# Gate and u projections of a two-layer encoder in pairs, by one level of Strassen

## The chip, the cores and the metric

The kernel runs on one core of a Trainium2 chip. The core has a matrix engine (TensorE, PE in the rows), a vector engine (VectorE, DVE), a scalar engine (ScalarE, ACT), GpSimd (POOL) and SyncE (SP), and 16 DMA engines that move data between DRAM and the on-chip memory. Each engine works off its own list of instructions in order. The metric is the device time of one execution in microseconds (us).

## The reference

There are two residual layers on an input of 512 rows by 2048 columns in float32. The first mixes a gated DeltaNet (a scan over chunks) with attention. The second, which the change rewrites, is this:

```python
def gmlp_layer(x, norm_g, w_in, ln_g, ln_b, w_s, b_s, w_out):
    h = rms_norm(x, norm_g)
    u, v, gate = jnp.split(h @ w_in, 3, axis=-1)            # w_in: 2048 x 6144
    u = jax.nn.gelu(u, approximate=False)
    v = layer_norm(jax.nn.gelu(v, approximate=False), ln_g, ln_b)
    vc = v.reshape(bsz, n, C_CHUNK, C_GROUPS, cg)           # 4 chunks of 128 rows, 16 groups of 128 columns
    s = jnp.einsum('gts,bnsgc->bntgc', w_s, vc) + b_s
    z = u * s.reshape(bsz, L, C_WIDTH) * jax.nn.silu(gate)
    return x + z @ w_out
```

## The kernel before

All large products are made in groups of 512 output columns (`proj`). A group holds 4 PSUM banks, one for each 128 rows of the input, and runs over 16 pieces of 128 weight rows. Every float32 operand is split in a high and a low part of a reduced format, so each piece and bank takes three matmuls: high with high, high with low, low with high. The high part of a weight piece is cast on ScalarE (`whi`), the low part is a subtraction on VectorE (`wlo`); `split(i)` makes both, `LOOK` = 2 pieces ahead of TensorE. The weights come from DRAM in slabs of 512 KB (two pieces), loaded by SyncE into `raw`, three buffers deep (`load_raw`).

The order on every engine is that in which the program records it. `proj` records three matmuls, and then `sub` lets the lanes `front`, `back` and `side` record some of the other work (generators; a positive yield is VectorE time in us, a negative one is a wait in ticks). One tick is three matmuls of 512 columns. `force` runs the lanes until a named thing is recorded.

The second layer is made of 4 groups VV (v), then for each of 4 column blocks a group GG (gate) and UU (u), and last 4 groups R (output). After UU of block j, `spatial(j)` mixes v over the rows in the lane: it turns `ws`, splits v, makes 12 matmuls (`sp`), multiplies into u and turns the result into `zT`. The first layer runs the scan from 400 to 650 us and the attention up to 800 us beside its projections, and its output groups O up to 1000 us. In the attention POOL does the rotary embedding (`rope`) of every head, at the end of which TensorE turns the head (`pq`), and `ro`, a power of -0.5 that VectorE waits for.

Of the kernel before, what the change touches and what calls it, by code (L numbers as in the profile page):

```python
# [14 lines left out]
P = 128  # L15
# [12 lines left out]
def encoder(ctx: ExitStack, tc: tile.TileContext, x, norm0_g, w_in0, conv0_w, a_log0, dt_bias0,  # L28
# [70 lines left out]
    x1_d = dr.tile([T, D], F32, name="x1_d")  # L99

# [47 lines left out]
    front, back, side = Lane(2), Lane(4), Lane(1)  # L148
# [21 lines left out]
    def sub(w, dve):  # L170

        dve *= w
        tick(w)
        if front.busy() and back.busy():
            f = 0.75 if ("scan", 1) in done else 0.35 if len(front.todo) <= 4 else 0.45 if "W" in done else 0.55
            front.run(f * dve, w)
            back.run((1.0 - f) * dve, w)
        else:
            front.run(dve, w)
            back.run(dve, w)  # L180
        side.run(1.0, w)

# [20 lines left out]
    for j in range(4):  # L203
# [5 lines left out]
    slabs = [(gi, q) for gi in range(len(groups)) for q in range(KT // 2)]  # L209
    raws, splits = {}, {}  # L210
    LOOK = 2

    def load_raw(qi):
        if qi >= len(slabs) or qi in raws:
            return
        gi, q = slabs[qi]
        _, w, c0, n, _ = groups[gi]
        raw = sb.tile([P, 2, 512], F32, tag="raw", bufs=3, name=uid("raw"))
        nc.sync.dma_start(raw[:, :, :n], w[q * 256:(q + 1) * 256, c0:c0 + n].rearrange("(a p) c -> p a c", p=P))
        raws[qi] = raw  # L220

    def split(i):
# [3 lines left out]
        n = groups[slabs[qi][0]][3]  # L226
        raw = raws[qi]
        hi = sb.tile([P, 512], F32R, tag="whi", bufs=LOOK + 1, name=uid("whi"))
        lo = sb.tile([P, 512], F32R, tag="wlo", bufs=LOOK + 1, name=uid("wlo"))
# [3 lines left out]
        if a == 0:  # L233
            load_raw(qi + 2)

# [8 lines left out]
    def proj(name, act, evac, first=None, late=None, func=None, tail=None):  # L244
        i0 = pos[0]
        nm, _, _, n, tr = groups[i0 // KT]
        assert nm == name, (nm, name)
# [53 lines left out]


# [36 lines left out]
    ssx = cst("ssx", [P, NT, 4])  # L339
    rs0 = cst("rs0", [P, NT])  # L340
# [32 lines left out]
    def start():  # L373
# [12 lines left out]
        nc.vector.tensor_scalar(rs0, rs0, 1.0 / D, EPS, ALU.mult, ALU.add)  # L386
        rsqrt(rs0, rs0)
        yield
# [836 lines left out]
    back.add(batch(), True)  # L1225
    proj("K0", act0, evac_conv("k", 0))
# [21 lines left out]
    h1_h, h1_l = [], []  # L1248
# [9 lines left out]
    def out0_group(j):  # L1258
        js = slice(j * 512, (j + 1) * 512)
        xr = []  # L1260
# [6 lines left out]
        def evac(t, pt):  # L1267
            z = xr[t]
            nc.vector.tensor_add(z, pt, z)
            spill(x1_d[t * P:(t + 1) * P, js], z)  # L1270
            jk = st("jk", [P, 512])
            nc.scalar.activation(jk, z, AF.Square, accum_out=ss1[:, t, j:j + 1])

        proj(f"O{j}", act_y, evac, late=load)
        front.add(h1_turn(j, xr))

    def h1_turn(j, xr):
        yield -2
        for a in range(4):
            k = j * 4 + a  # L1280
            if k % 8 == 0:
                h1_h.append(big("h1h", [P, 8, T], F32R))
                h1_l.append(big("h1l", [P, 8, T], F32R))
            pt = aux()
            for t in range(NT):
                transpose(pt[:, t * P:(t + 1) * P], xr[t][:, a * P:(a + 1) * P])
            hi = h1_h[k // 8][:, k % 8, :]
            g1 = cols[:, k:k + 1]
            nc.scalar.activation(hi, pt, AF.Copy, scale=g1)
            nc.vector.scalar_tensor_tensor(h1_l[k // 8][:, k % 8, :], pt, g1, hi.bitcast(F32), ALU.mult, ALU.subtract)  # L1290
            yield 0.6

    for j in range(4):
        out0_group(j)
    rs1 = cst("rs1", [P, NT])
    sm = tiny("sm", [P, NT])
    nc.vector.tensor_reduce(sm, ss1, AX.X, ALU.add)
    nc.vector.tensor_scalar(sm, sm, 1.0 / D, EPS, ALU.mult, ALU.add)
# [3 lines left out]
    act1 = act_in(h1_h, h1_l)  # L1302
    bst = sb.tile([P, 120], F32, tag="taps", bufs=1, name="bst")[:, 0:96].rearrange("p (t j s) -> p t j s", t=NT, j=4)
    vt = []

    def evac_v1(j):
        def f(t, pt):
            if not vt:
                vt.extend(big("vt", [P, 2, D]) for _ in range(2))
            z = vt[t // 2][:, t % 2, j * 512:(j + 1) * 512]  # L1310
            nc.scalar.activation(z, pt, AF.Gelu, scale=rs1[:, t:t + 1])
            front.add(stats(z, t, j))
        return f

    def stats(z, t, j):
        nc.vector.bn_stats(bst[:, t, j, :], z)
        yield 0.6

    for j in range(4):
        proj(f"VV{j}", act1, evac_v1(j), func=AF.Gelu if j == 0 else None)  # L1320

    def layer_norm1():
        lg = [[m4("lg", [P, 1024]) for _ in range(2)] for _ in range(2)]
        for i, src in enumerate((c_ln_g1, c_ln_b1)):
            for hf in range(2):
                nc.gpsimd.dma_start(lg[i][hf], src[0:1, hf * 1024:(hf + 1) * 1024].to_broadcast([P, 1024]))
        for t in range(NT):
            mv = tiny("mv", [P, 4])
            nc.vector.bn_aggr(mv[:, 0:2], bst[:, t].rearrange("p a b -> p (a b)"))
            nc.vector.tensor_scalar(mv[:, 2:3], mv[:, 1:2], EPS, None, ALU.add)  # L1330
            rsqrt(mv[:, 3:4], mv[:, 2:3])
            yield 1.0
            for hf in range(2):
                z = vt[t // 2][:, t % 2, hf * 1024:(hf + 1) * 1024]
                nc.vector.tensor_scalar(z, z, mv[:, 0:1], mv[:, 3:4], ALU.subtract, ALU.mult)
                yield 0.6
                nc.vector.tensor_mul(z, z, lg[0][hf])
                yield 1.1
                nc.vector.tensor_add(z, z, lg[1][hf])
                yield 1.1  # L1340

    front.add(layer_norm1())
    zT = [None, None]

    def gate_evac(sgs):
        def f(t, pt):
            if t % 2 == 0:
                sgs.append(m4("sg1", [P, 2, 512]))
            nc.scalar.activation(sgs[t // 2][:, t % 2, :], pt, AF.Silu, scale=rs1[:, t:t + 1])
        return f  # L1350

    def u_evac(us):
        def f(t, pt):
            if t % 2 == 0:
                us.append(m4("u1", [P, 2, 512]))
            nc.scalar.activation(us[t // 2][:, t % 2, :], pt, AF.Gelu, scale=rs1[:, t:t + 1])
        return f

    def spatial(j, us, sgs):
        ws = st("ws", [P, 4, P])  # L1360
        nc.gpsimd.dma_start(ws, c_ws1[0, j * 4:(j + 1) * 4].rearrange("g t s -> t g s"))
        for i in range(2):
            nc.vector.tensor_mul(us[i], us[i], sgs[i])
            yield 1.1
        yield 1.0
# [3 lines left out]
        wh = st("wh", [P, 4, P], F32R)  # L1369
        wl = st("wl", [P, 4, P], F32R)  # L1370
        pv = pw.rearrange("p (a t) -> p a t", a=4)
        nc.scalar.copy(wh, pv)
        nc.vector.tensor_sub(wl, pv, wh.bitcast(F32))
        yield 0.6
        vhl = {}

        def v_split(a):
            g = j * 4 + a
            cs = slice(g * P, (g + 1) * P)
            vh = st("vh", [P, NT, P], F32R)  # L1380
            vl = st("vl", [P, NT, P], F32R)
            for i in range(2):
                nc.scalar.copy(vh[:, 2 * i:2 * i + 2, :], vt[i][:, :, cs])
                nc.vector.tensor_sub(vl[:, 2 * i:2 * i + 2, :], vt[i][:, :, cs],
                                     vh[:, 2 * i:2 * i + 2, :].bitcast(F32))
            vhl[a] = (vh.rearrange("p n c -> p (n c)"), vl.rearrange("p n c -> p (n c)"))

        def z_out(a):
            g = j * 4 + a
            if g % 8 == 0:  # L1390
                zT[g // 8] = big("zT", [P, 8, T])
# [3 lines left out]
            nc.scalar.copy(zT[g // 8][:, g % 8, :], pz)  # L1395

        v_split(0)
        yield 0.7
        yield -2
        for a in range(4):  # L1400
            g = j * 4 + a
            vh2, vl2 = vhl.pop(a)
            sp = aux("sp")
            mm(sp, lhsT=wh[:, a, :], rhs=vh2, start=True, stop=False)
            mm(sp, lhsT=wh[:, a, :], rhs=vl2, start=False, stop=False)
            mm(sp, lhsT=wl[:, a, :], rhs=vh2, start=False, stop=True)
# [4 lines left out]
            if a < 3:  # L1411
                v_split(a + 1)
            yield 1.3
            z_out(a)
            yield 0.1
        done.add(("z", j))

    z_h, z_l, zs = [], [], {}

    def z_split(k):  # L1420
        if k < 2:
            z = m4("z01", [P, 2, T], F32R)
            zs[k] = z[:, 0, :], z[:, 1, :]
        else:
            i, j = divmod(k - 2, 8)
            if j == 0:
                z_h.append(big("zh", [P, 8, T], F32R))
                z_l.append(big("zl", [P, 8, T], F32R))
            zs[k] = z_h[i][:, j, :], z_l[i][:, j, :]
        hi, lo = zs[k]  # L1430
        src = zT[k // 8][:, k % 8, :]
        nc.scalar.copy(hi, src)
        nc.vector.tensor_sub(lo, src, hi.bitcast(F32))
        done.add(("zs", k))
# [87 lines left out]
```

## Time and profile before

| | us |
|---|---|
| median of three runs | 1739.9 (1739.77 to 1741.82) |
| the profiled execution | 1742.52 |
| its span, first to last instruction | 1740.7 |
| TensorE busy in the span | 1715.6 (99%) |
| VectorE busy | 869.2 (50%) |
| ScalarE busy | 701.9 (40%) |
| POOL busy | 155.1 (9%) |
| mean granted TensorE clock, share of full speed | 0.995 |

Matmuls overlap, so the busy time of one (about 0.39 us) is longer than the distance from one start to the next. The time that a matmul costs is that distance. DMA share is the mean busy share of the 16 DMA engines.

### The profile page before, as it was taken

To read this page: it belongs to the slowest core of one execution; us is meant where nothing else is said; L and a number is where in the kernel's file an instruction comes from. 1 tells how busy PE (TensorE), PEld (TensorE's weight loads), DVE (VectorE), ACT (ScalarE), POOL (GpSimd) and SP (SyncE) were. 2 spreads that over 40 slices of the span, in tenths; PEclk is the share of its full clock that TensorE was granted. 3 is DMA by queue.
4 is the path that set the end of the run, shared out by engine and by line. 5 is a ranking of instruction groups with operands and counts; after the bars stand their busy time and mean duration, and the time that the engine had idled before them with its cause. 6 is when DMAs were issued, how large, how long until landed. Compare 5 with 4: busy or idle time off the path is not lost.

```text
span 1740.7 us, 23332 instructions
## 1 busy us (share of the span) xinstructions
PE 1715.6 (99%) x8819; PEld 1406.4 (81%) x8819; DVE 869.2 (50%) x1570; ACT 701.9 (40%) x1423; POOL 155.1 (9%) x177
## 2 busy tenths in 40 slices
PE   9999999989999999999999999999999999999999
PEld 8887777767788998888788888888888888888887
DVE  4555588835765767875433332338342424245232
ACT  6443343524445556665433232223333434343221
POOL 0100200320000415440000000000000000000000
PEclk9999999989999999999999999999999999999999
DMA  6534553684546556435444443333333233333443
GB/s 193 141 95 123 131 126 90 167 193 139 151 136 159 151 140 198 136 94 173 157 135 139 121 161 97 97 88 107 97 91 96 80 92 94 94 118 109 136 140 103
DMA packets 166561, 221.36 MB, mean 127 GB/s; under 512 B 48546, under 2 KB 77522, under 8 KB 166449
## 3 DMA queue, kind: packets, MB, share of 16 engines
q1 hardware_dynamic: 161952, 207.27, 41.0%
q0 software_dynamic: 3744, 11.75, 3.0%
q8 instruction: 69, 1.13, 0.3%
q10 hardware_dynamic: 752, 0.86, 0.2%
q14 instruction: 44, 0.35, 0.1%
HBM read 186.18 MB, written 33.65 MB: 126 GB/s over the span
## 4 chain that ended last, share of the span: by engine, by line
PE 84%; issue 8%; DVE 3%; DMA 2%; ACT 2%; POOL 1%; SPq 0%; DVEq 0%; POOLq 0%; ACTq 0%
PE acc L276 20%; PE acc L275 20%; PE acc L277 20%; PE acc L271 5%; PE acc L272 5%; PE acc L273 5%; PE su L880 1%; PE po L1112 1%; DMA M<-e_d 1%; PE sc L849 1%; PE aux L84 1%; PE sc L876 1%; PE sc L862 1%; PE at L84 1%; PE sc L850 1%
## 5 line engine op out<-in xcount | busy, mean ns | idle before, releaser
L231 DVE TENSOR_TENSOR wlo<-raw,whi 128x512 fp32r<-128x512 f32 (+1 forms) x544 | 376.1, 692 | 750.9 <-ACT whi L230 745.0
L230 ACT CAST whi<-raw 128x512 fp32r<-128x512 f32 (+1 forms) x544 | 330.0, 607 | 743.9 <-PE acc L277 554.3
L275 PE MATMUL acc<-whi,h1h 128*128 128x512 f32 x768 | 304.5, 396 | 0.0
L277 PE MATMUL acc<-whi,h1l 128*128 128x512 f32 x768 | 303.3, 395 | 0.0
L276 PE MATMUL acc<-wlo,h1h 128*128 128x512 f32 x768 | 303.3, 395 | 0.0
L271 PE MATMUL acc<-hTh,whi 128*128 128x512 f32 x512 | 212.3, 415 | 0.9 <-DVE cs L509 0.9
L273 PE MATMUL acc<-hTh,wlo 128*128 128x512 f32 x512 | 204.0, 398 | 0.0
L272 PE MATMUL acc<-hTl,whi 128*128 128x512 f32 x512 | 203.7, 398 | 0.0
L277 PEld LDWEIGHTS acc<-whi,h1l 128*128 128x128 f32 x768 | 144.0, 187 | 35.1
L275 PEld LDWEIGHTS acc<-whi,h1h 128*128 128x128 f32 x768 | 144.0, 187 | 34.7
L276 PEld LDWEIGHTS acc<-wlo,h1h 128*128 128x128 f32 x768 | 144.0, 188 | 34.6
L275 PE MATMUL acc<-whi,hTh 128*128 128x352 f32 (+1 forms) x384 | 160.3, 417 | 1.6 <-ACT hTh L350 1.6
L277 PE MATMUL acc<-whi,hTl 128*128 128x352 f32 (+1 forms) x384 | 137.9, 359 | 0.3 <-DVE hTl L351 0.2
L276 PE MATMUL acc<-wlo,hTh 128*128 128x352 f32 (+1 forms) x384 | 137.9, 359 | 0.0
L273 PEld LDWEIGHTS acc<-hTh,wlo 128*128 128x128 f32 x512 | 97.0, 189 | 23.3
L271 PEld LDWEIGHTS acc<-hTh,whi 128*128 128x128 f32 x512 | 97.0, 189 | 21.4 <-DVE cs L509 1.5
L272 PEld LDWEIGHTS acc<-hTl,whi 128*128 128x128 f32 x512 | 97.4, 190 | 18.9
L275 PE MATMUL acc<-whi,zh 128*128 128x512 f32 x224 | 87.2, 389 | 0.0
L276 PE MATMUL acc<-wlo,zh 128*128 128x512 f32 x224 | 86.9, 388 | 0.0
L277 PE MATMUL acc<-whi,zl 128*128 128x512 f32 x224 | 86.9, 388 | 0.0
L277 PEld LDWEIGHTS acc<-whi,hTl 128*128 128x128 f32 x384 | 72.1, 188 | 9.6 <-DVE hTl L351 0.9
L275 PEld LDWEIGHTS acc<-whi,hTh 128*128 128x128 f32 x384 | 72.9, 190 | 7.5 <-ACT hTh L350 1.9
(323 smaller groups left out, 2393.8 us busy)
## 6 DMA issues: line engine op xcount, KB each, us to landing
raw<-in_w_in_dram SPq DMA_DIRECT2D x184, 512.0 KB, 3.9
raw<-in_w_out_dram SPq DMA_DIRECT2D x64, 512.0 KB, 3.7
kv<-kv_d SPq DMA_DIRECT2D x32, 256.0 KB, 3.9
raw<-in_w_in_dram SPq DMA_DIRECT2D x22, 352.0 KB, 3.9
kv_d<-nat SPq DMA_DIRECT2D x16, 256.0 KB, 4.2
TA<-u_d SPq DMA_DIRECT2D x64, 64.0 KB, 3.0
o_d<-ob SPq DMA_DIRECT2D x32, 128.0 KB, 4.5
xr<-in_x_dram SPq DMA_DIRECT2D x16, 256.0 KB, 5.0
```

The lines of the kernel that those rows point to most:

```text
L84: nc.tensor.transpose(out=o, in_=i, identity=ident[:k, :k])
L230: nc.scalar.copy(hi[:, :n], raw[:, a, :n])
L231: nc.vector.tensor_sub(lo[:, :n], raw[:, a, :n], hi[:, :n].bitcast(F32))
L271: mm(pt, lhsT=hi[:, s], rhs=ah, start=f, stop=False)
L272: mm(pt, lhsT=hi[:, s], rhs=al, start=False, stop=False)
L273: mm(pt, lhsT=lo[:, s], rhs=ah, start=False, stop=l)
L275: mm(pt, lhsT=ah[:, s], rhs=hi[:, cs], start=f, stop=False)
L276: mm(pt, lhsT=ah[:, s], rhs=lo[:, cs], start=False, stop=False)
L277: mm(pt, lhsT=al[:, s], rhs=hi[:, cs], start=False, stop=l)
L849: mm(pt[:, 0:128], lhsT=kq_chunk(h, cf), rhs=S[:, b, 0, :], start=True, stop=True)
L850: mm(pt[:, 128:256], lhsT=kq_chunk(h, cb), rhs=S[:, b, 1, :], start=True, stop=True)
L862: mm(pt[:, 256:384], lhsT=ta[:, 0, b, :], rhs=wk[:, 0, :], start=True, stop=True)
```

## The change

Let A be the normed input, cut in two halves of rows (256) and two of its 2048 columns (1024): A11, A12, A21, A22. For column block j, B has the gate columns on the left (B11, B21) and the u columns on the right (B12, B22), each 1024 by 512. The result of two groups (GG, UU) is now made of seven products of 256 by 1024 by 512 in place of eight, in the form of Winograd. The sums of A (S2, Sa, S3, S4) are made on VectorE during VV (`mixes`). The sums of B (T1 to T4) are made in DRAM: POOL issues 256 transfers of 256 KB, half of which copy and half of which add to what is there (`sums`), in a lane of its own, one per 3.9 ticks. The results are put together on VectorE (`combine`). For room, v and z now go through DRAM (`v_d`, `z_d`), and the layer norm of v is applied per group of 128 columns. The first-layer rows are scaled (`sc1`) before they are turned. `ex` is one large buffer, of which a part serves as fourth slab buffer; `wx` is a fourth pair of `whi`, `wlo`.

```diff
+    FAST = ("P1", "P2", "P6", "N5", "P7", "Q4", "N3")
-        group(f"GG{j}", wi1, 4096 + j * 512, 512)
-        group(f"UU{j}", wi1, j * 512, 512)
...
+        return [z[q] for q in ("B11", "B21", "T2", "T1", "T3", "T4", "B22")]
...
+            for z in range(LOOK + 2):
+                if z < LOOK + 1 or i + z >= 2 * F0 + 3 and i + z < 2 * F1:
+                    split(i + z)
...
+            for tb in range(2):
+                pt = home[o][tb]
+                ah, al = (a[:, w, tb * P:(tb + 1) * P] for w in range(2))
+                mm(pt, lhsT=ah, rhs=hi, start=k == 0, stop=False)
+                mm(pt, lhsT=ah, rhs=lo, start=False, stop=False)
+                mm(pt, lhsT=al, rhs=hi, start=False, stop=k == 7)
+                if tb == 0 and todo:
+                    evac(*todo.pop(0))
+                sub(1.0, 0.27)
...
+            if add:
+                nc.gpsimd.dma_start(tg_d[o][rs, c], s_, accum_op=ALU.add)
+            else:
+                nc.gpsimd.dma_start(tg_d[o][rs, c], s_)
+
+        STEPS = ((("T3", "B12", 0), ("T1", "B11", 0)), (("T3", "B22", 1), ("T1", "B12", 1)), (("T2", "T3", 0),),
+                 (("T2", "B11", 1),), (("T4", "T2", 0),), (("T4", "B21", 1),))
+        yield from until("A2")
+        yield -20
+        for n in range(len(rows) + len(STEPS) - 1):
+            for d, todo in enumerate(STEPS):
+                if 0 <= n - d < len(rows):
+                    for z in todo:
+                        move(n - d, *z)
+                        yield -3.9
...
+            if o == "P1":
+                into("X", banks)
+            elif o == "P2":
+                out("11", banks, "X", ALU.add)
+            elif o == "P6":
+                into("U2", banks, "X")
...
+            elif o == "P7":
+                into("U3", banks, "U2")
+                out("22", t["N5"], "U3", ALU.subtract)
+            elif o == "Q4":
+                out("21", banks, "U3", ALU.add)
+            else:
+                out("12", banks, "Y", ALU.add)
...
+        for n in range(NT):
+            nc.scalar.activation(vr[:, n, :], vr[:, n, :], AF.Identity, bias=nb[:, n:n + 1], scale=mv[:, 3, n:n + 1])
+        yield -1
+        for z, f in zip(lg, (ALU.mult, ALU.add)):
+            nc.vector.tensor_tensor(vr, vr, z[:, a * P:(a + 1) * P].unsqueeze(1).to_broadcast([P, NT, P]), op=f)
+            yield 0.7
+        nc.scalar.copy(g4(vh), vr)
+        yield -1
+        nc.vector.tensor_sub(g4(vl), vr, g4(vh).bitcast(F32))
...
-        proj(f"GG{j}", act1, gate_evac(sgs), func=AF.Silu)
-        proj(f"UU{j}", act1, u_evac(us), func=AF.Gelu, late=(lambda: (z_split(0), z_split(1))) if j == 3 else None)
+        fast(j, act2, combine(take_gu(sgs, us)),
+             late={"P6": lambda: front.add(prepare(3)), "N3": z_first} if j == 3 else {},
+             warms={"P2": AF.Silu, "P7": AF.Gelu, "Q4": AF.Silu, "N3": AF.Gelu})
         front.add(spatial(j, us, sgs))
 
 
+    z_firsts()
     back.add(z_splits())
```

On POOL, in the attention, these rows stand for the third query head before (`att` is the buffer of the rotary embedding, `r` and `ro` are the powers of -0.5 of the head and of the DeltaNet output):

```order
L998 TENSOR_TENSOR att_4972<-att_4972 128x512
L81 TENSOR_TENSOR ro_1039_6381<-ro_6348,nhalf 128x4
L1004 TENSOR_TENSOR att_4972<-att_4972 128x4x32 x4
L1007 TENSOR_TENSOR att_4972<-att_4972 128x512
L81 TENSOR_TENSOR r_6334<-r_6334,nhalf 128x4
L81 TENSOR_TENSOR ro_1053_6461<-ro_6441,nhalf 128x4
L1013 TENSOR_TENSOR att_4972<-att_4972,r_6334 128x512
```

and these for the same head now (L384 is an adding transfer, L386 a copy; `tgT_d` is any of T1 to T4):

```order
L1106 TENSOR_TENSOR att_5020<-att_5020 128x512
L81 TENSOR_TENSOR ro_1039_6455<-ro_6422,nhalf 128x4
L386 DMA tgT_d<-tgT_d 128x512
L1112 TENSOR_TENSOR att_5020<-att_5020 128x4x32 x4
L1115 TENSOR_TENSOR att_5020<-att_5020 128x512
L81 TENSOR_TENSOR r_6408<-r_6408,nhalf 128x4
L384 DMA tgT_d<-in_w_in_dram 128x512
L81 TENSOR_TENSOR ro_1053_6537<-ro_6516,nhalf 128x4
L1121 TENSOR_TENSOR att_5020<-att_5020,r_6408 128x512
```

The work of the head is unchanged, and two transfers have moved into it.

On VectorE, at the end of the last UU group and the start of R, these rows stand before (`wlo` is a low part of a weight piece, `z`, `zl` are low parts of the input of R):

```order
L231 TENSOR_TENSOR wlo_12895<-raw_12830,whi_12894 128x512
L1433 TENSOR_TENSOR z_2179_12900<-zT_11148,z_2179_12900 128x512
L1433 TENSOR_TENSOR z_2180_12903<-zT_11148,z_2180_12903 128x512
L231 TENSOR_TENSOR wlo_12919<-raw_12830,whi_12918 128x512
...
L231 TENSOR_TENSOR wlo_12988<-raw_12898,whi_12987 128x512
L231 TENSOR_TENSOR wlo_13022<-raw_12938,whi_13021 128x512
L1363 TENSOR_TENSOR u_2193_12994<-u_2193_12994,sg_2145_12705 128x1024
L1433 TENSOR_TENSOR zl_13034<-zT_11148,zh_13033 128x512
```

and these now (`chain` are the banks of the last product N3, `zl` as source is a piece of z read back from DRAM):

```order
L1588 TENSOR_TENSOR vx_13686<-ex_10943,vx_13686 128x512
L1541 TENSOR_TENSOR gu_13817<-chain_13722,pp_13496 128x512
L1541 TENSOR_TENSOR gu_13817<-chain_13723,pp_13497 128x512
L1573 TENSOR_TENSOR z_2388_13822<-zl_13718,z_2388_13822 128x512
L1573 TENSOR_TENSOR z_2389_13823<-zl_13720,z_2389_13823 128x512
L263 TENSOR_TENSOR wlo_13833<-raw_13764,whi_13832 128x512
L1573 TENSOR_TENSOR zl_13846<-zl_13841,zh_13845 128x512
```

The first two pieces of z, before split some pieces ahead of the end of UU, are now split behind the two rows that wait for the banks of N3.

On VectorE, at the end of the product P7 of block 3, where before only rows `wlo` stood at the end of a GG group, there are now these:

```order
L263 TENSOR_TENSOR wx_10872<-raw_13514,wx_10871 128x512
L1480 TENSOR_TENSOR pp_13383<-acc_13491,pp_13383 128x512
L1480 TENSOR_TENSOR pp_13384<-acc_13492,pp_13384 128x512
L1541 TENSOR_TENSOR gu_13611<-chain_13378,pp_13383 128x512
L1541 TENSOR_TENSOR gu_13611<-chain_13379,pp_13384 128x512
L263 TENSOR_TENSOR wlo_13627<-raw_13538,whi_13626 128x512
```

Four rows that read PSUM stand between two low parts.

## Rows read from the trace of the kernel before

**Rows 1.** The page, part 1: busy us, share of the span, instructions.
```profile
PE 1715.6 (99%) x8819; PEld 1406.4 (81%) x8819; DVE 869.2 (50%) x1570; ACT 701.9 (40%) x1423; POOL 155.1 (9%) x177
```

**Rows 2.** Windows by stage: length, engines busy (instructions), clock, DMA share, GB/s.
```profile
350.00:400.00 50.00, 42.44 (x648) 32.11 (x647) 15.87 (x19) 10.59 (x20) 10.65 (x14) 0.89 0.85 188
400.00:560.00 160.00, 156.56 (x819) 128.83 (x819) 100.59 (x249) 83.59 (x218) 0.00 (x0) 0.99 0.51 145
560.00:790.00 230.00, 226.67 (x1339) 200.66 (x1338) 172.35 (x372) 137.72 (x369) 89.06 (x98) 1.00 0.49 143
790.00:1001.00 211.00, 209.37 (x952) 169.09 (x951) 84.60 (x128) 78.76 (x150) 5.18 (x4) 0.99 0.47 147
1001.00:1180.00 179.00, 179.00 (x778) 143.90 (x776) 56.77 (x84) 53.40 (x86) 3.23 (x5) 1.00 0.36 110
...
1180.00:1554.00 374.00, 374.00 (x1637) 301.22 (x1636) 143.28 (x222) 129.85 (x219) 5.60 (x8) 1.00 0.32 96
```

**Rows 3.** Timeline of TensorE in VV: start us, us, engine, line, operation.
```profile
1201.00 0.40 PE L275 MATMUL acc<-whi,h1h 128*128 128x512 f32 x1
...
1203.80 0.40 PE L275 MATMUL acc<-whi,h1h 128*128 128x512 f32 x1
```

**Rows 4.** Timeline of ScalarE, then of VectorE, in GG and UU.
```profile
1408.48 0.62 ACT L230 CAST whi<-raw 128x512 fp32r<-128x512 f32 x1 [2.18 <-PE acc L277]
...
1409.13 0.69 DVE L231 TENSOR_TENSOR wlo<-raw,whi 128x512 fp32r<-128x512 f32 x1 [2.11 <-ACT whi L230]
```

**Rows 5.** Groups by line, 1180 to 1554 us: busy us, mean ns, idle before.
```profile
L275 PE MATMUL acc<-whi,h1h 128*128 128x512 f32 x512 | 203.0, 396 | 0.0
...
L231 DVE TENSOR_TENSOR wlo<-raw,whi 128x512 fp32r<-128x512 f32 x128 | 88.5, 691 | 208.9 <-ACT whi L230 208.5
L230 ACT CAST whi<-raw 128x512 fp32r<-128x512 f32 x128 | 79.4, 620 | 217.4 <-PE acc L277 215.2 <-DVE vt L1339 2.2
L1356 ACT ACTIVATE u<-acc,rs 128x512 f32<-128x512 f32 x16 | 11.0, 689 | 0.5
...
L1409 DVE SCALAR_TENSOR_TENSOR u<-sp,cols,u 128x256 f32<-128x256 f32 x24 | 10.5, 479 | 11.7 <-PE sp L1406 11.6
...
L1384 DVE TENSOR_TENSOR vl<-vt,vh 128x256 fp32r<-128x256 f32 x24 | 9.0, 417 | 0.0
...
L1363 DVE TENSOR_TENSOR u<-u,sg 128x1024 f32<-128x1024 f32 x6 | 7.1, 1217 | 0.0
```

**Rows 6.** Groups by line, whole span: an addition out of PSUM.
```profile
L1269 DVE TENSOR_TENSOR xr<-acc,xr 128x512 f32<-128x512 f32 x16 | 9.9, 682 | 0.0
```

**Rows 7.** The page, DMA: queue of POOL; issues, KB each, median us to landing.
```profile
q0 software_dynamic: 3744, 11.75, 3.0%
...
raw<-in_w_in_dram SPq DMA_DIRECT2D x184, 512.0 KB, 3.9
...
ws<-in_c_ws_dram POOLq DMA_DIRECT2D x4, 256.0 KB, 4.2
```

**Rows 8.** DMA issues from 350 to 400 us.
```profile
raw<-in_w_in_dram SPq DMA_DIRECT2D x6, 512.0 KB, 5.9
```

**Rows 9.** One issue on POOL: duration ns of `lg`; timeline of `M`.
```profile
L1326 POOL DMA_DIRECT2D lg<-in_c_ln_g_dram x2: 552/602/652, 1002.4 to 1003.1; - x2
...
338.79 1.17 POOL L762 DMA_DIRECT2D M<-e_d x1
```

**Rows 10.** Timelines of POOL, TensorE and VectorE around query heads in the attention.
```profile
678.39 1.21 POOL L81 TENSOR_TENSOR r<-r,nhalf 128x4 f32<-128x4 f32 x1
...
681.74 1.41 POOL L1013 TENSOR_TENSOR att<-att,r 128x512 f32<-128x512 f32 x1 [1.17 <-DVE r L1011]
...
686.67 0.60 PE L84 MATMUL pq<-ident,att 128*128 128x128 f32 x4
...
681.50 0.16 DVE L1011 TENSOR_SCALAR r<-r 128x4 f32<-128x4 f32 x1
...
718.27 1.52 DVE L1206 TENSOR_TENSOR ag<-ag,ro 128x512 f32<-128x512 f32 x1 [0.65 <-POOL ro L81]
```

More of the change, by code (lines that the diff above doesn't have):

```diff
@@ L215, in load_raw @@
             return
[L216 to L219, printed above, removed]
+        src, n = slabs[qi]
+        if FR <= qi < F1 and (qi - FR) % 4 == 3:
+            ex(0)
+            raw = ex_[0][:, 0:2, :]
+        else:
+            raw = sb.tile([P, 2, 512], F32, tag="raw", bufs=3, name=uid("raw"))
+        nc.sync.dma_start(raw[:, :, :n], src.rearrange("(a p) c -> p a c", p=P))
         raws[qi] = raw
@@ L225, in split @@
         qi, a = divmod(i, 2)
-        n = groups[slabs[qi][0]][3]
+        n = slabs[qi][1]
         raw = raws[qi]
-        hi = sb.tile([P, 512], F32R, tag="whi", bufs=LOOK + 1, name=uid("whi"))
-        lo = sb.tile([P, 512], F32R, tag="wlo", bufs=LOOK + 1, name=uid("wlo"))
+        if F0 <= qi < F1 and (i - 2 * F0) % 4 == 3:
+            if not wx_:
+                wx_.extend(st("wx", [P, 512], F32R) for _ in range(2))
+            hi, lo = wx_
+        else:
+            hi = sb.tile([P, 512], F32R, tag="whi", bufs=LOOK + 1, name=uid("whi"))
+            lo = sb.tile([P, 512], F32R, tag="wlo", bufs=LOOK + 1, name=uid("wlo"))
         nc.scalar.copy(hi[:, :n], raw[:, a, :n])
@@ L1225, in encoder @@
     back.add(batch(), True)
+    mem.add(sums())
     proj("K0", act0, evac_conv("k", 0))
@@ L1319, in encoder, with take_gu, take @@
+    def take_gu(sgs, us):
+        def take(c, tb, pt, y, f):
+            dst = us if c[1] == "2" else sgs
+            h = c[0] == "2"
+            if h not in dst:
+                dst[h] = m4("gu", [P, 2, 512])
+            z = dst[h][:, tb, :]
+            nc.vector.tensor_tensor(z, pt, y, op=f)
+            t = tb + 2 * h
+            nc.scalar.activation(z, z, AF.Gelu if c[1] == "2" else AF.Silu, scale=rs1[:, t:t + 1])
+        return take
+    back.add(mixes())
     for j in range(4):
         proj(f"VV{j}", act1, evac_v1(j), func=AF.Gelu if j == 0 else None)
[L1322 to L1340, printed above, removed]
@@ L1359, in spatial, with z_home @@
[L1359 to L1365, printed above, removed]
+    stored("v1")
+    front.add(layer_norm1())
+    force("mixes")
+    z_h, z_l, zs = [], [], {}
+    def z_home(k):
+        if k in zs:
+            return zs[k]
+        if k < 2:
+            if 0 not in zs:
+                z = [m4("z01", [P, 2, T], F32R) for _ in range(2)]
+                zs[0], zs[1] = ((y[:, 0, :], y[:, 1, :]) for y in z)
+        else:
+            i, j = divmod(k - 2, 8)
+            while len(z_h) <= i:
+                z_h.append(big("zh", [P, 8, T], F32R))
+                z_l.append(big("zl", [P, 8, T], F32R))
+            zs[k] = z_h[i][:, j, :], z_l[i][:, j, :]
+        return zs[k]
@@ new lines, in v_load, with mixing @@
+    def v_load(j, a):
+        z = g4(ex(5 + a % 2))
+        nc.sync.dma_start(z, v_d[j * 4 + a])
+        return z
+    def mixing(j):
+        yield from until("v1", "ln")
+        lg = [st("lg", [P, 512]) for _ in range(2)]
+        for z, src in zip(lg, (c_ln_g1, c_ln_b1)):
+            nc.gpsimd.dma_start(z, src[0:1, j * 512:(j + 1) * 512].to_broadcast([P, 512]))
+        ws = g4(ex(4))
+        nc.sync.dma_start(ws, c_ws1[0, j * 4:(j + 1) * 4].rearrange("g t s -> t g s"))
+        vr = v_load(j, 0)
+        yield -6
```

335 lines of the change are left out of this document (243 added, 92 removed).

## The prediction

> **What bounds the kernel now.** I read the busy times first, then the windows by stage, then the timeline of one stage. TensorE is busy for 99% of the span [rows 1]. From 1000 us on it has no gap at all: 179.00 of 179.00 us in VV, 374.00 of 374.00 in the four blocks of GG and UU that the change rewrites [rows 2]. There the matmuls start at a fixed distance: from 1201.00 to 1203.80 us lie 12 of them, 0.2333 us each [rows 3]; the 0.396 us of a group row is the length of one, two of which overlap. The other engines have room. Per weight piece (2.80 us) ScalarE works 0.62 us and waits 2.18 us for TensorE, VectorE works 0.69 us and waits 2.11 us [rows 4]. VectorE is busy 143 of 374 us and the DMA engines 0.32 of the time. So in this stage a matmul less is worth 0.2333 us, as long as pieces of weights still arrive in time.
>
> **What goes.** Per column block GG and UU have 2 x 16 x 4 x 3 = 384 matmuls, the seven products have 7 x 8 x 2 x 3 = 336. Four blocks lose 192, and the order on TensorE is shorter by exactly that number; turns and mixing matmuls stay. 192 x 0.2333 = 44.8 us. No other edit takes anything from TensorE.
>
> **What the pace of the pieces becomes.** A weight piece now serves 6 matmuls, 1.40 us in place of 2.80, so everything per piece has half the time. VectorE per block: 56 low parts x 0.691 = 38.7 us [rows 5], 14 additions out of PSUM x 0.682 = 9.5 us [rows 6], and `spatial`: two products of u and gate 2.4, eight updates of u 3.8 [rows 5], 13 operations of 512 columns for ws and v at 0.69, 9.0. That is 63.4 of 56 x 1.40 = 78.4 us, 81%. ScalarE: 56 casts x 0.620 = 34.7, eight activations x 0.689 = 5.5 [rows 5], 11 further casts and copies 6.8, and sixteen short pieces of the norm at less than a cast each, under 9.9: 73% beside four table loads. Both fit on average. The question is the bursts, since each engine keeps its order. Pieces are split three ahead. At the end of a product VectorE has one low part (1.4 us after TensorE began the next product), two additions (2.8) and perhaps one row of the lane (3.5); ScalarE, behind two activations, casts the next piece by 4.1, its low part ends at 4.8, and TensorE wants it at 5.6: no wait. At P7 there are four additions (the rows in the order on VectorE): the same count ends at 6.2, 0.6 us late. Four times that is 2.4 us; where the lane puts ScalarE work between, some tenths more; and the turn of `ws` stands 6 ticks (4.2 us) behind its load, which lands in 4.2 us [rows 7] and later when the DMA is fuller. I take 5 us for the four blocks. Bounds: 0, and 16 if each of the 28 product ends loses 0.6.
>
> **The end of the blocks.** Before, z 0 and 1 were split beside UU. Now they are split behind the last results of N3. After its last matmul VectorE adds the second bank (0.7), ScalarE finishes its activation (1.6) and casts z 0 (2.2), VectorE makes its low part (2.9): TensorE stands about 2.5 us, and the next pieces, read back from DRAM in place of `zT`, may hold a cast for a while. I take 3.5 us, bounds 2 and 7.
>
> **The sums in DRAM.** Their order on POOL says when they go: 38 transfers before the first rotary row (560 us), 45 up to 790, 71 up to the norm of layer 2 (1001), 64 in VV, 30 in block 0, 8 after. No transfer from DRAM to DRAM and no adding one is in this trace. A copy of 262,144 bytes takes 0.87 us of all 16 engines at the rate of the weight loads (96 GB/s at 0.32, so 300 GB/s at full share) [rows 2], 1.16 us at that of POOL's queue (11.75 MB in 3.0% of the span, 225 GB/s) [rows 7]. An add I put between a copy and twice one: a mean transfer of 0.87 to 1.75 us; I take 1.31 (copy 0.87, add twice that), nearest to the weight loads, since the rows are 2 KB in both. With the share of each stage [rows 2] that gives, low to high: 0.72 to 0.93 until 560 us, 0.66 to 0.83 in the attention, 0.76 to 1.06 in O, 0.67 to 0.99 in VV. Weight loads have slack there: three buffers of 5.6 us each, and at a share of 0.85 they land in 5.9 us [rows 8] where 3.9 is usual [rows 7]. So I price these stages at 0 for the weights. Block 0 is the tight one: its weights alone, 28 slabs in 78.4 us, are 187 GB/s, share 0.62, and 30 transfers make it 0.95 to 1.29, 1.12 by my value. Load slack is six pieces, 8.4 us, against an excess of 0.12 x 78 = 9 us, which the two queues share. I take 4 us, bounds 0 and 20.
>
> Here a page can be weighed. The trace has no row for an add. The Trainium skill (Collectives: The Full Stack, section "The bandwidth ceiling: the fold count and why AG ≠ RS ≠ AR") says that a reducing transfer is slow because it needs two source reads, and gives 32.35 against 62.28 GB/s for the plain one. No run shown here bears this out yet. By it block 0 is over-subscribed and pays the 4 us; were an add as cheap as a copy, it would not pay, and the sum were 4 us better.
>
> **POOL in the attention.** Nothing of the sums waits on TensorE, but POOL issues them between the steps of a head. One issue takes 0.60 us for 128 rows, 1.17 us for many small pieces [rows 9]. One or two stand within a head. From POOL's last step to the turn on TensorE there are 3.5 us (681.74 + 1.41 to 686.67), from its power to the VectorE row that needs it 1.9 us (678.39 + 1.21 to 681.50), but at `ro` VectorE already waits, 0.65 us [rows 10]. Behind that wait stand all low parts and the softmax. Eight heads and eight `ro` with 0.6 to 1.2 us, about a third of it reaching TensorE: 4 us, bounds 0 and 19 (16 x 1.2). POOL has at most eight transfers open (each waits for the eighth before it); at 4 us apart that is some 30 us for one to land. The loads of `yb` and of DeltaNet's output before O come later by some of this contention: 2 us, bounds 0 and 8.
>
> Free: the sums of A on VectorE during VV, 8 x (10 x 0.42 + 1.2) = 43 us where 57 of 179 us are taken [rows 2, 5]; without that cover they would delay P6 by as much. The scaled copies in O go to ScalarE, which is busy 79 of 211 us there; without that cover, 16 x 0.69 = 11 us.
>
> **Sum.** -44.8 + 5 + 3.5 + 4 + 4 + 2 = -26.3 us. The profiled execution took 1742.52, 1.8 over its span and 2.6 over the median; 1739.9 - 26.3 is 1714. With all lower bounds (only 2 us lost) it is 1697, with all upper ones, 70 us, it is 1765.
>
> **Rivals.**
> My forecast, 1697 to 1737 us, has 0.70.
>
> First rival, slower: an add costs far more than two copies. From 400 to 1258 us the engines have 452 us free (one minus the share, stage by stage) [rows 2]. 248 transfers fit as long as they take 1.82 us on average. What is over lengthens the program, because POOL holds at its eight open transfers, the heads wait for POOL and TensorE for the heads. The gain is gone at 478 us, 1.93 us on average: an add of 2.7 us beside a copy of 1.16. At three copies (3.5 us) the mean is 2.33, 126 us over, and the time 1840. For it: nothing like it has been measured here. Against: the order spaces transfers by about 4 us in the attention, so POOL rarely has more than a few open. Chance 0.16.
>
> Second rival, no gain or little: the paired products run at the pace of VectorE and ScalarE, not of TensorE. At 81% busy with three pieces of lookahead the bursts may cost 1.2 to 1.6 us at each of 28 ends, 34 to 45 us in place of 5: 1743 to 1754 with the rest. Against: the count above closes with 0.8 us to spare at six of seven ends. Chance 0.10, half of it at or above the time before.
>
> Third, all is hidden but the end of the blocks: 1697. Chance 0.04.
>
> Within 0.2% (3.5 us, what a measurement of this kernel can tell) lie only the edges of these: 0.05. Faster: 0.73, slower 0.22. The likeliest range is 1697 to 1737; 8 in 10 is 1697 to 1765.
>
> **What would show it.** Right: the stage of the four blocks takes 374 - 44.8 + 5 to 10 us, matmul starts stay 0.2333 us apart, waits of TensorE there name `wlo` behind P7, one gap of 2 to 4 us stands before R, and the stage up to 1001 us grows by less than 10 us. Adds would land in under 15 us. Wrong: a DMA share at 0.95 and above from 400 us on with POOL waiting for its own transfers, raw loads that land in over 8 us, or TensorE waits at every product end.

## The result and the profile after

The changed kernel takes 1825.7 us (median, 1821.3 to 1827.3), the kernel before 1739.8 us in the same comparison: a ratio of 1.049, interval 1.047 to 1.052. The forecast was 1714 us, with 1697 to 1765 as the range. It is wrong in its sign.

The profiled execution has a span of 1823.4 us against 1740.7. Two lines of its page answer to [rows 1, 7]: TensorE's busy time, and the queue of POOL (packets, MB, share of the 16 engines):

```profile
PE 1711.1 (94%) x8627; PEld 1384.5 (76%) x8627; DVE 1008.7 (55%) x1819; ACT 808.7 (44%) x1627; POOL 327.6 (18%) x431
...
q0 software_dynamic: 32160, 77.82, 20.0%
```

TensorE has its 192 matmuls less and still stands idle for 112 us of the span (25 before). Where, the same windows as in [rows 2] tell, cut at the same work (from the DeltaNet scan to the end of the paired blocks):

```profile
352.00:408.00 56.00, 43.14 (x647) 32.77 (x646) 15.22 (x19) 10.78 (x20) 19.29 (x27) 0.87 1.00 209
408.00:586.00 178.00, 161.61 (x823) 132.63 (x823) 100.88 (x251) 83.27 (x218) 18.18 (x27) 0.95 0.67 178
586.00:828.00 242.00, 230.92 (x1337) 203.59 (x1337) 185.12 (x373) 137.46 (x369) 125.05 (x153) 0.99 0.75 193
828.00:1052.00 224.00, 210.99 (x941) 168.36 (x940) 85.00 (x138) 87.30 (x166) 46.61 (x65) 0.98 0.74 210
1052.00:1254.00 202.00, 183.71 (x786) 146.71 (x785) 97.02 (x179) 66.37 (x109) 44.95 (x65) 0.96 0.73 188
1254.00:1633.00 379.00, 348.40 (x1447) 266.00 (x1445) 228.06 (x365) 215.59 (x385) 32.40 (x47) 0.99 0.71 213
```

Every stage is longer, those that the change was not meant to touch above all, and the DMA share is nowhere above 0.75 but in the first. In windows of 50 us it looks different (the share adds up the times of packets, so it can pass 1):

```profile
400.00:450.00 50.00, 36.79 (x164) 29.40 (x164) 20.60 (x48) 17.55 (x46) 23.50 (x34) 0.86 1.07 264
450.00:500.00 50.00, 42.89 (x215) 34.21 (x216) 30.67 (x74) 22.91 (x58) 0.00 (x0) 0.93 0.58 151
...
1000.00:1050.00 50.00, 47.84 (x212) 38.10 (x211) 16.90 (x28) 18.77 (x37) 0.00 (x0) 1.00 0.41 127
...
1100.00:1150.00 50.00, 33.81 (x137) 26.55 (x136) 24.93 (x49) 11.96 (x18) 22.97 (x34) 0.83 1.07 257
```

The share is 1.07 in two of these windows and 0.41 or 0.58 in the two others, and POOL has work in the full ones only. POOL's timeline shows why (start, us, engine, line; in brackets the idle time before and what ended it):

```profile
385.82 2.59 POOL L890 DMA_DIRECT2D u_d<-W  x4 [26.86 <-ACT W L884]
...
393.65 2.12 POOL L386 DMA_DIRECT2D tgT_d<-in_w_in_dram  x4
400.55 0.88 POOL L384 DMA_DIRECT2D tgT_d<-in_w_in_dram  x1 [4.78 <-DMA tgT_d<-in_w_in_dram]
...
1057.82 1.03 POOL L81 TENSOR_TENSOR rs<-sm,nhalf 128x4 f32<-128x4 f32 x1 [90.54 <-DVE sm L1444]
1058.83 1.73 POOL L384 DMA_DIRECT2D tgT_d<-in_w_in_dram  x2
```

POOL waits for another engine (27 us for `W`, 91 us for `sm`), and then everything behind it in its order leaves at once, held only by its own eight open transfers. 38 transfers go in the 50.4 us from 393.65 on, 61 in 107 us of O, 64 in 87 us of VV, 38 in 73 us of block 0; the other 55 go in the attention, 43 of them with at most two others open. The loads of weights share the engines with these clumps. From 400 to 450 us they take this long to land (count, KB each, median us; 5.9 in [rows 8], 3.9 in [rows 7]):

```profile
raw<-in_w_in_dram SPq DMA_DIRECT2D x5, 512.0 KB, 20.4
```

In VV the chain of waits goes through two such loads, one behind the other:

```profile
1100.97 38.65 DMA raw<-in_w_in_dram x2
```

In the blocks a second thing is seen. Beside the late weights TensorE stands at the matmuls of `spatial`, which need the normalized `v` (VectorE, ScalarE and TensorE around one of them):

```profile
1389.21 0.62 ACT L1586 CAST vh<-ex 128x512 fp32r<-128x512 f32 x1 [1.58 <-DVE ex L1584]
...
1390.99 0.69 DVE L1588 TENSOR_TENSOR vl<-ex,vh 128x512 fp32r<-128x512 f32 x1
...
1391.73 0.50 PE L1665 MATMUL sp<-vl,wh 128*128 128x512 f32 x1 [1.35 <-DVE vl L1588]
...
1633.30 0.80 PE L308 MATMUL acc<-whi,z 128*128 128x512 f32 x1 [3.92 <-ACT z L1572]
```

The matmul stands right behind the lines that make `vl`, VectorE makes it behind another low part, and TensorE waits 1.35 us for it with the next products behind. The last row is the forecast gap at the end of the blocks.

### The profile page after: what moved, and what is told of

Same layout as the page of the kernel before. It is cut to its first block, busy times and chain, and to the rows that moved or that the text cites. A ratio compares the mean times of both kernels' runs of the same rounds, so it can differ in the third digit from the quotient of the medians.

```text
span 1823.4 us, 24045 instructions
## 1 busy us (share of the span) xinstructions
PE 1711.1 (94%) x8627; PEld 1384.5 (76%) x8627; DVE 1008.7 (55%) x1819; ACT 808.7 (44%) x1627; POOL 327.6 (18%) x431
## 3 DMA queue, kind: packets, MB, share of 16 engines
q0 software_dynamic: 32160, 77.82, 20.0%
## 4 chain that ended last, share of the span: by engine, by line
PE 69%; DMA 15%; DVE 7%; ACT 5%; issue 4%; POOL 1%; SPq 0%; ACTq 0%; DVEq 0%; POOLq 0%
PE acc L308 11%; PE acc L309 11%; PE acc L310 11%; PE acc L304 6%; PE acc L305 5%; PE acc L306 5%; DMA raw<-in_w_in_dram 4%; DMA raw<-tgT_d 3%; DMA raw<-in_w_out_dram 3%; DVE wlo L263 2%; PE acc L358 2%; PE acc L359 2%; PE acc L357 2%; ACT whi L262 1%; PE chain L359 1%
## 5 line engine op out<-in xcount | busy, mean ns | idle before, releaser
L263 DVE TENSOR_TENSOR wlo<-raw,whi 128x512 fp32r<-128x512 f32 (+1 forms) x557 | 396.3, 716 | 628.7 <-ACT whi L262 616.7
L262 ACT CAST whi<-raw 128x512 fp32r<-128x512 f32 (+1 forms) x557 | 333.8, 606 | 611.4 <-PE acc L310 274.3
L384 POOL DMA_DIRECT2D tgT_d<-in_w_in_dram x128 | 114.9, 935 | 129.0 <-DMA tgT_d<-in_w_in_dram 94.3
L308 PE MATMUL acc<-whi,opA 128*128 128x512 f32 x256 | 101.9, 398 | 16.2 <-ACT whi L262 16.2
L309 PE MATMUL acc<-wlo,opA 128*128 128x512 f32 x256 | 102.5, 400 | 0.0
L310 PE MATMUL acc<-whi,opA 128*128 128x512 f32 x256 | 101.4, 396 | 0.0
L309 PEld LDWEIGHTS acc<-wlo,hTh 128*128 128x128 f32 x384 | 73.1, 190 | 5.3
L552 DVE SCALAR_TENSOR_TENSOR cv<-cs,taps,cv 128x510 f32<-128x510 f32 (+1 forms) x96 | 73.1, 763 | 0.8 <-ACT cv L547 0.4
## 6 DMA issues: line engine op xcount, KB each, us to landing
tgT_d<-in_w_in_dram POOLq DMA_DIRECT2D x192, 256.0 KB, 11.5
```

The lines of the kernel that those rows point to most:

```text
L262: nc.scalar.copy(hi[:, :n], raw[:, a, :n])
L263: nc.vector.tensor_sub(lo[:, :n], raw[:, a, :n], hi[:, :n].bitcast(F32))
L308: mm(pt, lhsT=ah[:, s], rhs=hi[:, cs], start=f, stop=False)
L309: mm(pt, lhsT=ah[:, s], rhs=lo[:, cs], start=False, stop=False)
L310: mm(pt, lhsT=al[:, s], rhs=hi[:, cs], start=False, stop=l)
L384: nc.gpsimd.dma_start(tg_d[o][rs, c], s_, accum_op=ALU.add)
```

## The experiments

The first theory from these rows was: clumps of transfers that starve the weight loads (A). Its rival: the paired products run at the pace of VectorE and ScalarE (B). The table has what the runs gave by stage, in us between the first matmuls of the stages on TensorE's timeline, R up to its last matmul (before and in e1, GG begins with the 257th matmul of `whi` with `h1h`).

```
run                     median   to O     O      VV    blocks   R
before                  1739.8   807.0  192.0  180.9   373.2  183.6
changed                 1825.7   844.9  207.5  202.0   378.9  186.4
e1 sums alone           1781.1   833.5  204.0  180.9   373.2  183.6
e2 no sums              1749.3   813.0  200.3  183.7   360.7  186.1
e3 copies for adds      1786.8   823.2  204.2  194.6   369.1  186.3
e4 paced                1755.7   818.4  200.0  183.7   363.1  185.6
e5 + late turns         1748.7   820.9  193.2  181.5   359.5  185.5
e6 + late spatial       1735.8   816.4  193.1  181.5   343.5  194.5
e7 spacing 4.6          1761.6   819.0  195.3  181.5   376.2  185.3
e8 early start          1758.2   835.8  193.1  181.5   344.1  194.0
e9 all                  1723.0   816.3  193.9  181.5   337.8  187.7
e10 all, no sums        1717.7   813.6  192.6  181.5   336.8  188.4
e11 all, unpaced        1794.7   845.1  200.9  201.1   356.4  188.4
e12 all, copies         1717.8   814.2  193.0  181.5   335.7  187.7
```

**e1, the sums alone in the kernel before.**

```
+    front, back, side, mem = Lane(2), Lane(4), Lane(1), Lane(1)
+    mem.add(sums())          # beside back.add(batch(), True)
```

> The kernel before, with the 256 transfers of the sums added at the same places and read by nothing; its matmuls are those of before. Theory A (clumps): on POOL long runs of transfers stand between two waits for other engines, so they leave in four clumps at the pace of their own queue, the weight loads of these stretches land three to five times later, and TensorE waits. Then the sums alone cost the 74 us that the changed kernel had lost by the start of its blocks, and some 5 to 10 us more where the fourth clump meets the first group of GG: 1740 + 74 + 8 = 1822 us, range 1805 to 1835. Theory B (the paired products themselves cost the time, the transfers are hidden): within 10 us of 1740.

1781.1 us, half of the loss foreseen and outside the range of 1805 to 1835. To the start of VV the clumps cost 38.5 us (53.4 in the changed kernel, of which 14.3 are there without any transfer, e2). Under VV and GG the same clumps cost nothing, with the DMA engines as full as in the changed kernel:

```profile
1040.00:1100.00 60.00, 60.00 (x267) 48.31 (x266) 20.70 (x30) 19.70 (x32) 29.32 (x42) 1.00 1.06 263
```

There the weights are the only other traffic and land in 9.3 us, while a piece serves 2.8 us and the buffers hold three slabs of two pieces. VV of the changed kernel has the same pace, and there too loads land in 9 to 11 us and TensorE hardly waits, until the first store of `v` at 1100.52. From 1100 to 1150 us, beside these stores, it reads:

```profile
raw<-in_w_in_dram SPq DMA_DIRECT2D x6, 512.0 KB, 19.9
...
v_d<-v SPq DMA_DIRECT2D x4, 256.0 KB, 25.5
```

The clumps that cost time in e1 have a third stream beside them as well: the scan's own loads at 400 us (weights land in 15 us), the loads and stores of the residual rows in O (17 us). So A holds, and its price is that of the stage that the clump meets: nothing beside weights at 2.8 us a piece, 10 us and more of waits where a third stream runs. That the third stream makes the difference is read from these traces; no run takes the stores of `v` alone away.

**e2, no sums.**

```
-    mem.add(sums())
+    done.update(("sums", j) for j in range(4))
-    ... ("B11", "B21", "T2", "T1", "T3", "T4", "B22")
+    ... ("B11", "B21", "B12", "B12", "B22", "B21", "B22")
```

> The changed kernel without any transfer of the sums: the seven products read quarters of the weights themselves in place of T1 to T4, so the sums are left out of the result; loads, splits, matmuls and additions keep their number and sizes. Theory A: the 74 us ahead of the blocks go, and block 0 falls from 111 us to the 91 of the later blocks less their beginnings; the blocks then take about 78.4 + 3 x 91 = 351 to 360 us against 373 before, and with 2.4 us behind them the time is 1722 to 1732, I take 1728. Theory B: the blocks still take 379 us, and the time is 1745 or more.

1749.3 us, outside A's 1722 to 1732: 76 us less than the changed kernel, and still no gain on the kernel before. The blocks take 360.7 us, at the upper edge of what A has, but the rest doesn't follow. A alone does not do. The waits of TensorE (line, releaser; us, times, longest) name the rest:

```profile
PE sp L1665 <- DVE vl L1588: 9.2, 12, 1.3
PE aux L84 <- ACT xs L1380: 5.8, 8, 1.0
PE acc L308 <- ACT z L1572: 3.9, 1, 3.9
...
PE aux L84 <- DVE opA L1413: 2.6, 4, 0.7
PE pw L84 <- DMA ex<-in_c_ws_dram: 2.1, 3, 0.8
```

`xs` and `opA` are the turns of the O groups, which now need four scaled copies from ScalarE first: O and VV take 11.1 us more than before. In the blocks each matmul's distance to the next, less 0.2333, sorted by what the row names, adds up to 33.0 us: 11.5 at `vl`, 6.2 at `whi` and `wlo`, 4.1 at `z`, 2.5 at `ws`, 1.6 at `vh`, and 7.1 on slow matmuls behind such waits that name nothing.

**e3, copies in place of adds.**

```
-    nc.gpsimd.dma_start(tg_d[o][rs, c], s_, accum_op=ALU.add)
+    nc.gpsimd.dma_start(tg_d[o][rs, c], s_)
```

> The changed kernel with each of the 128 adding transfers turned into a plain copy of the same source, target and place, so the sums are left out of the result. Theory A: a packet of an add took 225 ns in the changed kernel and one of a copy 204 ns, so the clumps are nearly as long, and the time is 1805 to 1822 us. Rival (an add is what is dear, the first rival of the prediction): the loss of 83 + 45 us falls by about half or more, 1765 us or less.

1786.8 us, below A's range and above the rival's: of the loss of 128 us, 39 go. The packets of 204 ns were the adds, those of 225 ns the copies and other transfers of the queue, and an add takes twice as many packets as a copy. The share of POOL's queue settles the price:

```profile
q0 software_dynamic: 23968, 77.82, 14.9%
```

It was 3.0% of 1740.7 us before [rows 7], 52 us. Here 14.9% of 1781.1 are 265 us, so a copy takes (265 - 52) / 256 = 0.83 us of all 16 engines. In the changed kernel 20.0% of 1823.4 are 365 us, 99 more for 128 adds: an add takes 0.83 + 0.78 = 1.61 us, 1.9 times a copy. The packets say the same: 32160 against 23968 are 64 more for each add. So the clumps get shorter without adds (64 transfers in 65 us of VV in place of 87), and so does the loss.

**e4, paced.** VectorE writes a column at the place of each transfer, and POOL copies it before it issues; all else is the changed kernel.

```
+            tk = sb.tile([P, 1], F32, tag="tk", bufs=16, name=uid("tk"))
+            nc.vector.memset(tk, 0.0)
+            nc.gpsimd.tensor_copy(pk, tk)
             if add:
```

> The changed kernel with each transfer held back on POOL until VectorE has reached its place: VectorE writes one column ahead of each, POOL copies it before it issues. Same transfers, same order, 256 small pieces of work more on VectorE. Theory A: POOL no longer runs ahead, the transfers are spread at some 3 us, weight loads land in 5 to 8 us, most of the 74 us ahead of the blocks goes: 1740 to 1770 us. Rival (it is the amount: 256 transfers and the weight loads don't fit in these stretches however they are spread): the loss only moves, 1800 us or more.

1755.7 us, 70 us less, within the range. POOL now stands in front of each transfer and lets one go every 2.8 us here (3.6 us as a mean of all):

```profile
901.87 0.18 POOL L387 COPY pk<-tk 128x1 f32<-128x1 f32 x1 [1.52 <-DVE tk L386]
902.31 0.82 POOL L389 DMA_DIRECT2D tgT_d<-in_w_in_dram  x1 [0.26 <-issue]
904.67 0.18 POOL L387 COPY pk<-tk 128x1 f32<-128x1 f32 x1 [1.54 <-DVE tk L386]
```

and the same transfers fit beside the weights, in windows that are alike from 850 to 1200 us (0.79 to 0.87), with loads that land in 4.4 us as a median of the whole run:

```profile
900.00:950.00 50.00, 47.90 (x213) 38.14 (x212) 17.03 (x44) 18.90 (x37) 14.23 (x33) 1.00 0.84 213
...
1100.00:1150.00 50.00, 50.00 (x216) 40.21 (x215) 24.40 (x62) 15.81 (x24) 16.20 (x36) 1.00 0.86 213
```

```profile
raw<-in_w_in_dram SPq DMA_DIRECT2D x157, 512.0 KB, 4.4
tgT_d<-in_w_in_dram POOLq DMA_DIRECT2D x192, 256.0 KB, 5.4
```

**e5, late turns.**

```
     def h1_turn(j, xs):
-        yield -2
+        yield -6
```

> The paced kernel, with the turns of each O group emitted four positions of the order later. Theory: without any sums the O groups still lose 12.4 us, because TensorE meets the turns before ScalarE has made the four scaled copies and their four squares; four positions (2.8 us) later the copies are there. 1756 - 12 = 1744 us, range 1741 to 1749. Rival (ScalarE is full at a group's end, so the wait comes back at the next cast or turn): 1752 us or more.

1748.7 us, at the upper end of the range, 7 of the 12 us: O falls from 200.0 to 193.2, VV from 183.7 to 181.5.

**e6, late spatial.**

```
-        yield -6             # mixing, ahead of the turn of ws
+        yield -9
+            yield -2         # ahead of sp = aux("sp")
```

> As the one above, and in the paired blocks the three matmuls of spatial stand two positions behind the low part of v that they read, the turn of ws three positions later. Theory: of the 8 to 9 us that a block loses without any sums, these waits (0.9 + 1.35 + 0.4 + 0.4 us for the low part of v, 0.8 for ws, and the slow matmuls behind each) are about 5; three blocks and a part: 13 to 15 us less than the kernel above, 1730 us, range 1726 to 1737. Rival (VectorE and ScalarE are full in a block, whatever the order): less than 5 us less.

1735.8 us, inside the range, and the first kernel here under the one before (ratio 0.998, interval 0.996 to 0.999). The blocks give back 16 us, R loses 9: the last block's rows now come late, since its `spatial` got the two positions as well.

**e7 and e8, transfers over a longer time.** In e7 `yield -4.6` in place of `-3.9`; in e8 `yield -5.6`, and no `until("A2")` at the start.

> As e6, with 4.6 in place of 3.9 positions between two transfers, so that they end in block 2 and not at the end of block 0. If the DMA load is what is left of the loss, attention, O and block 0 give back 3 to 8 us: 1722 to 1728. If spread transfers cost next to nothing already: within 2 us of e6. If the last transfers now come late for their block: slower than e6 by 5 us or more.

> As e6, with the transfers begun at the start of the program and 5.6 positions apart. If the DMA load from the attention to block 0 is what is left of the loss: 4 to 10 us less than e6. Rival: in DeltaNet POOL's small pieces now stand behind held transfers, each of them up to some us late on the chain that TensorE waits for, and the start loses more than the rest gains: slower than e6.

Both are slower, 1761.6 and 1758.2 us: in e7 the last of its three cases, in e8 the rival. In e7 the sums of the last block are not yet issued where block 3 begins in the order; `force(("sums", 3))` then writes out what is due, and the lanes with it, so that all of block 2's `spatial` stands ahead of block 3 with no product between its steps. TensorE takes it step by step, 8 us each:

```profile
1461.60 0.80 PE L1670 MATMUL sp<-vh,wh 128*128 128x512 f32 x1 [4.38 <-ACT vh L1591]
...
1469.61 0.79 PE L1670 MATMUL sp<-vh,wh 128*128 128x512 f32 x1 [4.37 <-ACT vh L1591]
```

In e8 the start of the program loses: O begins 19.4 us later than in e6. The longest wait of TensorE up to there is one for POOL's paced queue, in front of a small piece of DeltaNet:

```profile
PE mg L884 <- POOL pk L387: 10.1, 1, 10.1
```

**e9, all.** e6 with `spatial` put in order once more, and e10, the same without sums.

```
-            yield -2         # ahead of sp = aux("sp")
+            if j < 3:
+                yield -4
             ...
             yield 0.1        # behind z_out(a)
-            yield -2
+            if j == 3:
+                yield -2
             ...              # the last block's parts of v, ahead of its own loop
+            nx = v_load(j, a + 1) if a < 3 else None
             yield from v_parts(j, a, vr, lg, vx[:, 2 * a, :], vx[:, 2 * a + 1, :])
-            if a < 3:
-                vr = v_load(j, a + 1)
-                yield -5
+            vr = nx
```

> e6 with the order of spatial changed once more: in blocks 0 to 2 its matmuls stand four positions behind the low part of v (two in e6), the two positions at the end of a step go, the last block's part gets none, and its parts of v are loaded one ahead. In e6 the stage of the output projection took 194.5 us where the changed kernel took 186.4, because the last block's rows came late, and waits for vh and vl still cost 7 us. Both gone: 1736 - 8 - 5 = 1723 us, range 1718 to 1730. If ScalarE and VectorE are full in a block whatever the order: 1734 us or more.

> e9 without any transfer of the sums (the products read quarters of the weights, the sums are left out of the result). What it takes less than e9 is the price of 256 spread transfers. By the stages of e2 and e4 (attention and before 5 us, block 0 2.4 us): 6 to 8 us less than e9, 1716 us. If spread transfers were free it would be equal to e9; if most of the remaining loss is theirs, 1705 us or less.

1723.0 us, as expected, 0.990 of the kernel before (interval 0.988 to 0.992): the version that beats both. Without any sums it is 1717.7 us, so spread transfers cost 5.3 us, a little under the 6 to 8 expected. In e9 O, VV and the blocks read:

```profile
816.00:1010.00 194.00, 190.13 (x850) 152.13 (x849) 76.76 (x186) 78.79 (x149) 62.70 (x132) 1.00 0.88 239
1010.00:1191.00 181.00, 180.64 (x783) 145.27 (x782) 98.10 (x242) 66.39 (x108) 59.59 (x129) 1.00 0.83 209
1191.00:1529.00 338.00, 332.20 (x1448) 265.08 (x1446) 225.22 (x402) 215.74 (x381) 46.97 (x87) 1.00 0.77 240
```

A DMA share of 0.88 as a mean over a whole stage, and TensorE busy for 98% of it; the changed kernel had 0.74 and 94%.

**e11 and e12, one part of e9 undone.** e11 drops the three lines of the pacing, e12 makes the adds copies.

> e9 with the pacing alone taken out: its transfers leave POOL as in the changed kernel. If the clumps cost what e4 gave back (70 us), they cost it here too: 1723 + 70 = 1793 us, range 1775 to 1805. If most of what e4 gave back came from where other waits fell and not from the pacing: 1750 us or less.

> e9 with the 128 adding transfers as plain copies, paced (the sums are left out of the result). In clumps an add cost more than a copy: in VV 64 copies of e3 left in 64 us, 65 transfers of the changed kernel, half of them adds, in 87 us, so an add took the queue some 1.65 times a copy. If that matters only where the queue is full, spread ones take the same as e9 within 3 us. If an add is dear of itself, this is 4 to 5 us faster than e9, all that e10 gave.

1794.7 us without the pacing: the clumps cost 71.7 us here as they cost 70.0 in the changed kernel. 1717.8 us with copies, as much as with no transfers at all: the second of the two cases, all that the spread sums still cost, 5 us, goes with the adds.

## Why the prediction was wrong

**The step that failed** is "Their order on POOL says when they go", and what was built on it, "So I price these stages at 0 for the weights". The prediction spread each stage's transfers evenly over the stage. An order says what comes before what. When an instruction goes is said by what it waits for, and between two of POOL's waits nothing held the transfers but each other. How many go in a stage came out nearly right (38, 55, 61, 64 and 38 against 38, 45, 71, 64 and 38), and so did the mean shares of the stages (0.75 in the attention, 0.73 in VV; 0.74 in O, a little under the forecast); inside a stage they went in clumps. The rows were there: POOL in VV busy 3.23 of 179 us in [rows 2] has nothing to be held by. "The order spaces transfers by about 4 us in the attention" was nearer the truth: there POOL has the heads to wait for, and 43 of 55 transfers went with at most two others open. Price of the clumps: 70 to 72 us (e4, e11), where 10 us were put down for block 0, the heads and the loads before O together, and 5.3 us when the spacing is real (e9 less e10). POOL's own hold at eight open transfers, which the first rival named, kept the queue full, but heads that wait for POOL can be no more than the 12 us that the attention lost; VV and the blocks have no heads, and each took 18 us more than without transfers (e2). The prediction's own signs of being wrong were there in the first trace: a share of 1.07 from 400 to 450 us, and weight loads that land in 20 us.

**A term left out**: `spatial`. The prediction added up its work on VectorE and ScalarE (81 and 73% busy) and looked for waits at product ends alone. But its matmuls stand in TensorE's order a fixed number of positions behind the lines that feed them; with both engines busier (VectorE 228 of 379 us in the blocks against 143 of 374, ScalarE 216 against 130) these lines finish later than their place. From e5 to e9 the blocks fall from 359.5 to 337.8 us by moving these places and, for the last block, loads of `v`.

**An edit priced at nothing that wasn't**: the scaled copies in O. ScalarE had room as a mean, but at a group's end it makes four copies and four squares in a row, and the turns wanted the copies at once. O and VV lost 11.1 us by it in e2, which is the prediction's price without cover (11 us); e5 took 7.1 us off the time by moving the turns (9.0 us off these two stages).

**What held.** The gain of 44.8 us is there: the blocks of e10 take 336.8 us against 373.2 - 44.8 = 328.4. By the count of e2, e10 loses 9.4 us in them: 4.1 are the gap at `z` (3.5 foreseen), 1.5 stand at `whi` and `wlo` (5 foreseen for the product ends), 1.5 at `vl`, 2.3 on slow matmuls behind them. The price of the transfers held too: 0.87, twice that for an add, 1.31 as a mean were put down; 0.83, 1.61 and 1.22 were measured. That an add is twice a copy was a guess between two bounds, taken before any row of an add. The Trainium skill (Collectives: The Full Stack, section "The bandwidth ceiling: the fold count and why AG ≠ RS ≠ AR") gives 62.28 GB/s for an AllGather and 32.35 for a ReduceScatter among four ranks, a ratio of 1.93, and lays it to the two source reads of an add; the runs here have nearly the same ratio, 1.61 / 0.83 = 1.9, and do not show whether its reason is the same. The first rival's condition, an add far over two copies, was therefore not met, and its 452 us of free engine time were enough once the transfers were spread.

The second rival gave 1743 to 1754 us with the sums hidden, and e2 measured 1749. The number is right and the mechanism is not: of the 33.0 us lost in the blocks of e2 only 6.2 stand at `whi` and `wlo`; the rest is order, and e10 has the same work on the same engines and loses 9.4 us by the same count. It was luck.

**Open**: 6 to 7 us to the start of O in e2 and e10, which have no transfers; up to there they run the code of before but for a few small operations at the start. All of it is there already at the first `sc` of the scan (398.3 us before; 5.9 us later in e2, 6.4 in e10). Runs of the same code differed from it by -3.1 (e1) to +2.8 us (e2) at 363 us, so about half may be spread between executions. It was not settled.

## What to carry to other kernels

A transfer's place in an engine's order is no time: between two waits of the issuing engine everything leaves at once, so read from the trace what that engine will be waiting for, and where it waits for nothing, give each transfer something to wait for (here one column from VectorE, 0.18 us on POOL). Where work is taken off the bounding engine, count not only whether its helpers still fit on average, but for each instruction placed at a fixed distance in its order whether its input is still ready at that distance. Judge DMA room in windows as short as the buffers (here some 15 us of weights), not by the mean of a stage, and there by how late the loads land against what the buffers cover: at a share of 1.06 with loads in 9.3 us nothing was lost (e1), at 1.07 with loads in 20 us 16 us of waits came in 50.

## What the runs showed of the hardware that I had not expected

Eight open transfers of 256 KB from DRAM to DRAM slow a 512 KB load on another queue from 3.9 to 9.3 us (VV of e1), and to 15 to 20 us where a third stream runs too; one transfer each 2.8 us slows it to 4.8 beside the same stores of `v` (VV of e4). VV with a DMA share of 0.83 from end to end loses nothing (181.5 us in e9 and in e10), with 0.73 in clumps it loses some 20 us (202.0 in the changed kernel, 201.1 in e11). Spread, 256 copies cost nothing that could be measured (e12 against e10), and 128 adds in place of half of them 5 us (e9 against e12). And the granted clock makes each wait dearer: behind the long waits it falls to the lower of its two levels (1.2 GHz; in VV from 1127 to 1144 us), which gives means of 0.83 and 0.86 in the windows shown, and matmuls start 0.43 us apart for some 1 to 5 us before they return to 0.2333.
